# A value projection as seven products and a written order of steps in a two-layer mLSTM and attention trunk

## The chip, the cores and the metric

The kernel runs on one core of a Trainium2 chip. The metric is the device time of one execution in microseconds (us), the median of several runs. TensorE (PE in the profile) multiplies, VectorE (DVE), ScalarE (ACT) and GpSimd (POOL) work on rows of 128 partitions, and SyncE (SP) and GpSimd issue the transfers from HBM.

## The reference, cut to what matters

Two layers, each of three blocks, on 256 tokens of width 1024 in float32; every block ends in a layer norm of the residual sum.

```python
for l in range(2):
    x = layer_norm(ALPHA * x + 0.5 * swiglu(x, ffn_w_in[l, 0], ffn_w_out[l, 0]), ...)   # F = 2816
    y = mlstm_mixer(x, ...) if l == 0 else window_attention(x, ...)
    x = layer_norm(ALPHA * x + y, ...)
    x = layer_norm(ALPHA * x + 0.5 * swiglu(x, ffn_w_in[l, 1], ffn_w_out[l, 1]), ...)

def mlstm_mixer(x, w_in, gate_b, norm_g, w_out):      # 4 heads, q and k 128 wide, v 256 wide
    p = x @ w_in                                      # columns: q 512, k 512, v 1024, o 1024, gates 16
    h = mlstm(q, k, v, gates forward) + mlstm(..., backward)   # decay weights exp(...), read |den| with a floor
    h = normalised per head * norm_g
    return (sigmoid(o) * h) @ w_out
```

The value projection is `x @ w_in[:, 1024:2048]`, the output gate `o` is `x @ w_in[:, 2048:3072]`.

## The kernel before

Every float32 product is made of three float32r matmuls: weights and activations are split in a high part (ScalarE's cast, `w_hi`) and a low part (VectorE's subtraction, `w_lo`), and `mm3` adds hi·hi, hi·lo and lo·hi in one PSUM bank. A word of weights is 128 x 1024; it comes by one transfer of 512 KB and needs one cast on ScalarE and one subtraction on VectorE before TensorE can use it.

The program is written once as a list of steps on tiles without addresses (`Book.note`). `Book.sequence` then plans it: TensorE's steps keep the order in which they were written; the steps of VectorE, ScalarE, GpSimd and of the transfers are picked by due times, with costs from `Book.cost` and a small model of the two transfer rings (`Rings`, `RING`). It also picks the slots of the tiles. `emit` writes the result, one queue in order for each engine; so nearly all rows of the profile have one line, L597, and are told apart by the tiles' names. A step that needs a set of ScalarE's function tables comes behind a `preload` step in the list; after the plan, the lowering puts a table load of its own wherever an activation stands behind a load of another set.

The feed-forward blocks (`ffn`) take most products 512 columns at a time for gate and up part together, as seven products instead of eight (`seven`): words of weights are summed on VectorE or by accumulating transfers from GpSimd's queue (`bring`), sums of the transposed x (`x_one` to `x_four`) are made once, and the seven products `P1`, `P2`, `S1` to `S4`, `A22` share three banks. The strings `FIRST`, `FULL`, `SHUT` and `OPEN` give the order of these steps (`d`, `a` and `b` are products of the down projection and of the rest of 256 columns).

The mLSTM block (`mlstm`) runs in this order: the value projection as 32 groups of three matmuls (`wide_mm`, then `v_evac`), with the transposes of the previous block's second half (`pending`) inside; the gates' projection and their scans; q and k (`narrow`); then for each head `scores`, `mix`, `divide`, `settle`, with the output gate's 32 groups (`gate_units`, counts in `GATE`) between them; `gate_out`, the transposes of the gated h (`to_xT`), and the out projection with the norm (`tail`, `Norm`). ScalarE's tables are loaded in four places there: Exp and Ln ahead of the gates, Sigmoid ahead of the output gate, Silu at the end, and Exp again in the attention block. In this block's names `wt` are the decay weights of a head (six Exp steps of 128 x 128 each), `a` their product with the scores, `den` the denominators, `sg` the sigmoid, `py` and `pw` banks of PSUM.

The attention block (`attn`) follows the string `HEADS`: `P`, `S`, `E`, `N`, `T`, `V` with a pair of heads' number are products, scores, powers, scale, transposes and values, `q*n` and `y0*n`, `y1*n` are n groups of the q projection and of the out projection of each half of the tokens.

Layer norms of the feed-forward blocks other than the last are seeded: ScalarE writes the scaled residual to the bank ahead of the products (`seed`), the products add to it, and ScalarE copies the sum out with a running total (`half`). Mixers and the last block add the residual on VectorE.

Of the kernel before, what the change touches and what calls it, by code (L numbers as in the profile page):

```python
# [27 lines left out]
SUMS = {(2, 0): "23", (5, 0): "23"}  # L28
# [221 lines left out]
class Book:  # L250
# [170 lines left out]
    def sequence(self):  # L421
# [54 lines left out]
        while len(given) < len(steps):  # L476
# [124 lines left out]
def trunk_kernel(ctx: ExitStack, tc: tile.TileContext, x, ffn_w_in, ffn_w_out, ln_g, ln_b, ml_w_in, ml_gate_b,  # L601
# [156 lines left out]
    class Norm:  # L758
        def __init__(self, t, ca, eps, last=False, seeded=False):
            self.t, self.ca, self.eps, self.last, self.seeded = t, ca, eps, last, seeded  # L760
            if last:
# [4 lines left out]
            if not last:
                self.sums = small("sums", [128, 6])
# [58 lines left out]
    def tail(y, h, todo, first, norm, last, turn_at, between=None):  # L826

        def one(t, o, n):
            c, get = todo[t][n]
# [31 lines left out]
        return lambda: emit_x(1, last)  # L861

    def ffn(l, i, n, pending, last):
# [68 lines left out]
        xs, f1 = {}, {}  # L932

        def x_sum(name, a, op, b):
            f = temp(name).rearrange("p (k m) -> p k m", k=4)
            nc.vector.tensor_tensor(f, a, b, op=op)
            v = nc.tile(name, (128, 2, 4, 128), "wide" if name in ("S1", "S2") else "big", FR)
            xs[name] = (v[:, 0], v[:, 1])
            split_evac(xs[name], f)
            return f  # L940

        def x_one():
            f1["x"] = temp("x10").rearrange("p (k m) -> p k m", k=4)
            nc.scalar.copy(f1["x"], turned[1, 0])
            f1["S1"] = x_sum("S1", f1["x"], OP.subtract, turned[1, 1])

        def x_two():
            f1["S2"] = x_sum("S2", f1["S1"], OP.subtract, turned[0, 0])

        def x_three():  # L950
            x_sum("S3", turned[0, 0], OP.subtract, f1["x"])

        def x_four():
            x_sum("S4", turned[0, 1], OP.add, f1["S2"])

# [659 lines left out]
```

## Time and profile before

| what | value |
|---|---|
| time, median of 3 runs | 906.04 us (904.73 to 907.65) |
| profiled execution: time, span | 904.83 us, 903.1 us |
| PE busy | 892.5 us, 99% |
| DVE, ACT, POOL busy | 815.9 us (90%), 635.1 us (70%), 157.8 us (17%) |
| transferred | 216.92 MB, mean 240 GB/s |
| granted TensorE clock | 0.999 |
| ScalarE table loads | 6, 1283 ns each |

The span runs from the first to the last instruction. Matmuls are pipelined and their ends are modelled, so a PE that reads as busy can still have stood for up to a few tenths of a us: such stops show in the starts of the rows, since a 128 x 512 matmul follows the one before by 0.227 us. By the starts, the blocks begin at about 0, 173, 299, 453, 637 and 722 us, and the last matmul starts at 895.4 us.

### The profile page before, as it was taken

The page shows a single profiled execution, that of the slowest core. Times are in us where ns is not written, and L with a number is a line of the kernel's source. Part 1 is how long each engine was busy: PE and PEld are TensorE (multiplying, and loading weights), DVE is VectorE, ACT ScalarE, POOL GpSimd, SP SyncE. Part 2 cuts the span into 40 slices and gives each one's busy share as a digit, 9 for nine tenths or more (in the row PEclk, how much of TensorE's full clock was granted, in tenths as well). Part 3 has the DMA queues.
Part 4 walks back from the last instruction along what each step waited for, and adds up shares of the span by engine and source line. Part 5 has one row for each costly group of instructions (what it writes and reads, how often), then busy time and mean ns, then how long its engine had stood idle before and what let it go on. Part 6 is the DMA issues. An engine that isn't in the chain of part 4 may idle for free.

```text
span 903.1 us, 12618 instructions
## 1 busy us (share of the span) xinstructions
PE 892.5 (99%) x4387; PEld 744.3 (82%) x4387; DVE 815.9 (90%) x1008; ACT 635.1 (70%) x881; POOL 157.8 (17%) x194
## 2 busy tenths in 40 slices
PE   9999999999999999999999999999999999999996
PEld 7888888889988888888888888887898788888885
DVE  7999998678797999999879999996889899999975
ACT  7777677657665886776679776776788777677650
POOL 0121221014012221112011221131033131112100
PEclk9999999999999999999999999999999999999999
DMA  9999998844395989999966999999534588999931
GB/s 317 380 306 273 274 317 243 293 141 141 119 315 149 212 241 316 300 249 278 363 185 177 244 291 322 295 258 347 168 113 113 168 191 230 306 267 263 307 90 46
DMA packets 106111, 216.92 MB, mean 240 GB/s; under 512 B 7192, under 2 KB 23600, under 8 KB 106048
## 3 DMA queue, kind: packets, MB, share of 16 engines
q1 hardware_dynamic: 84000, 174.09, 54.6%
q0 software_dynamic: 22048, 42.04, 27.1%
q8 instruction: 34, 0.56, 0.2%
q14 instruction: 29, 0.24, 0.1%
HBM read 215.04 MB, written 1.05 MB: 239 GB/s over the span
## 4 chain that ended last, share of the span: by engine, by line
PE 73%; DVE 11%; issue 9%; DMA 5%; ACT 1%; POOL 1%; DVEq 0%; POOLq 0%; ACTq 0%
PE pw L597 45%; PE py L597 28%; DVE w_lo L597 5%; DMA b<-in_ffn_w_in_dram 5%; DVE b L597 2%; DVE x L597 1%; DVE e L597 1%; ACT w_hi L597 1%; POOL b L597 1%; POOL rs L597 1%; DVE S L597 0%; DVE xT_lo L597 0%; DVE pv L597 0%; DVE sc L597 0%; DVE h_lo L597 0%
## 5 line engine op out<-in xcount | busy, mean ns | idle before, releaser
L597 ACT CAST w_hi<-b 128x1024 fp32r<-128x1024 f32 x266 | 277.6, 1053 | 98.6 <-PE py L597 45.4
L597 DVE TENSOR_TENSOR w_lo<-b,w_hi 128x1024 fp32r<-128x1024 f32 x266 | 317.5, 1220 | 9.9 <-ACT w_hi L597 9.8
L597 DVE TENSOR_TENSOR w_lo<-raw,w_hi 128x1024 fp32r<-128x1024 f32 (+1 forms) x158 | 187.4, 1208 | 10.5 <-ACT w_hi L597 9.1
L597 PE MATMUL pw<-w_hi,S 128*128 128x512 f32 x608 | 195.3, 391 | 0.2 <-ACT e L597 0.2
L597 ACT CAST w_hi<-raw 128x1024 fp32r<-128x1024 f32 (+1 forms) x158 | 163.2, 1042 | 44.3 <-PE py L597 19.1
L597 POOL DMA_DIRECT2D b<-in_ffn_w_in_dram x80 | 97.0, 1218 | 497.4 <-DVE b L597 173.8
L597 PE MATMUL pw<-w_hi,xT_hi 128*128 128x512 f32 (+1 forms) x420 | 164.9, 394 | 0.4 <-ACT xT_hi L597 0.4
L597 PE MATMUL pw<-w_hi,xT_lo 128*128 128x512 f32 (+1 forms) x420 | 162.4, 388 | 0.0
L597 PE MATMUL pw<-w_lo,xT_hi 128*128 128x512 f32 (+1 forms) x420 | 161.2, 387 | 0.0
L597 PEld LDWEIGHTS pw<-w_hi,S 128*128 128x128 f32 x608 | 114.2, 188 | 25.0 <-ACT e L597 0.7
L597 PE MATMUL py<-w_hi,h_hi 128*128 128x512 f32 x317 | 125.7, 397 | 0.0
L597 PE MATMUL py<-w_hi,h_lo 128*128 128x512 f32 x317 | 124.0, 391 | 0.6 <-DVE h_lo L597 0.6
L597 PE MATMUL py<-w_lo,h_hi 128*128 128x512 f32 x317 | 123.5, 390 | 0.0
L597 PE MATMUL pw<-w_lo,S 128*128 128x512 f32 x304 | 118.4, 390 | 0.0
L597 PEld LDWEIGHTS pw<-w_hi,xT_lo 128*128 128x128 f32 x420 | 78.9, 188 | 18.3 <-DVE xT_lo L597 2.1
L597 PEld LDWEIGHTS pw<-w_hi,xT_hi 128*128 128x128 f32 x420 | 79.0, 188 | 16.2 <-ACT xT_hi L597 1.4
L597 PEld LDWEIGHTS pw<-w_lo,xT_hi 128*128 128x128 f32 x420 | 78.9, 188 | 14.6
L597 DVE TENSOR_TENSOR b<-b,b 128x1024 f32<-128x1024 f32 x72 | 87.7, 1221 | 0.7
L597 PEld LDWEIGHTS py<-w_hi,h_lo 128*128 128x128 f32 x317 | 59.5, 188 | 13.7 <-DVE h_lo L597 1.0
L597 PEld LDWEIGHTS py<-w_lo,h_hi 128*128 128x128 f32 x317 | 59.7, 188 | 11.8
L597 PEld LDWEIGHTS py<-w_hi,h_hi 128*128 128x128 f32 x317 | 59.6, 188 | 11.6
L597 PEld LDWEIGHTS pw<-w_lo,S 128*128 128x128 f32 x304 | 57.1, 188 | 11.6
(205 smaller groups left out, 1102.3 us busy)
## 6 DMA issues: line engine op xcount, KB each, us to landing
b<-in_ffn_w_in_dram SPq DMA_DIRECT2D x152, 512.0 KB, 7.9
raw<-in_ffn_w_out_dram SPq DMA_DIRECT2D x88, 512.0 KB, 8.2
b<-in_ffn_w_in_dram POOLq DMA_DIRECT2D x80, 512.0 KB, 8.8
raw<-in_ml_w_in_dram SPq DMA_DIRECT2D x24, 512.0 KB, 8.0
raw<-in_ffn_w_in_dram SPq DMA_DIRECT2D x36, 256.0 KB, 6.3
raw<-in_at_w_in_dram SPq DMA_DIRECT2D x12, 512.0 KB, 8.6
raw<-in_ml_w_out_dram SPq DMA_DIRECT2D x8, 512.0 KB, 4.5
raw<-in_at_w_out_dram SPq DMA_DIRECT2D x8, 512.0 KB, 8.4
```

Source lines behind the costliest of these rows:

```text
L597: getattr(engines[s.engine], s.name)(*[real(x) for x in s.args], **{k: real(x) for k, x in s.kw.items()})
```

## The change

Five edits:

1. `seven` is cut into a function `strassen` that both `ffn` and `mlstm` use. The value projection becomes one block of seven products over all 1024 columns, with sums of x from `sums_of_x`. Two of the word sums come by accumulating transfers (`SUMS`, entry `(1, 0)`), two on VectorE; four more words are brought by accumulating transfers.
2. The mLSTM's steps follow a string `MIXES`. The output gate's first 16 groups (`u`) move to the front, among the value products; their result is copied out unchanged and passed through Sigmoid later (`sig`). The q and k groups are taken head pair by head pair, and scores and mixes start inside them.
3. `Norm` is seeded in the mixers too (attention: the first half of the tokens) and in the last block for the first half.
4. `HEADS`, `SHUT` and `OPEN` are changed in a few places.
5. Constants of the plan: `RING`, a new `SPARE` added to landing times, `SUMMED`, and costs of some steps.

```diff
-SUMS = {(2, 0): "23", (5, 0): "23"}
+SUMS = {(1, 0): "01", (2, 0): "23", (5, 0): "23"}
-HEADS = ('... E7 y0*2 N7 y0*1 V5 y1*1 '
-         'T60 T61 y0*1 y1*1 V6 y1*1 T70 y1*1 T71 y1*1 V7 y0*1 y1*1 y0*3')
+HEADS = ('... E7 y0*2 '
+         'N7 V5 y1*1 T60 T61 y0*2 y1*1 V6 T70 y1*1 T71 y1*2 V7 y0*1 y1*1 y0*3')
-GATE = [4, 4, 4, 4, 4, 10, 2]
+MIXES = ('P1*2 u*4 P2*2 u*2 p u*2 x1 u*4 x3 g x2 u*4 x4 S1*2 S2*2 S4*2 S3*2 q*7 A22*2 q*1 c q*29 '
+         'sig q*1 H0 q*2 H1 q*8 M0 q*16 u*2 H2 M1 u*1 H3 u*3 M2 u*2 M3 u*8')
-SHUT = "P1*2 d T1 P2*2 S1*2 S2*2 d S3*2 S4*2 d A22*2 T0"
+SHUT = "P1*2 d T1 P2*2 S1*2 S2*2 d*2 S3*2 S4*2 A22*2 T0"
-RING = {"SP": (2000.0, 600.0), "POOL": (2900.0, 1500.0)}
+RING = {"SP": (2000.0, 1250.0), "POOL": (2900.0, 1150.0)}
+SPARE = {"SP": 300.0, "POOL": 1500.0}
-SUMMED = 163.0
+SUMMED = 170.0
...
             if s.name.startswith("preload"):
-                s.takes = 1290.0
+                s.takes = 1450.0
...
-                        steps[n_].lands = t_
+                        steps[n_].lands = t_ + SPARE[steps[n_].engine]
...
     class Norm:
-        def __init__(self, t, ca, eps, last=False, seeded=False):
+        def __init__(self, t, ca, eps, last=False, seeded=True):
+            self.parted = last and t
+            self.seeded = seeded and not self.parted
...
     def mlstm(l, n, pending, last):
...
-        wide_mm(ps[0], 0, wv, 0)
-        v_evac(0, 0, ps[0])
...
+        todo_ = strassen(ml_w_in[0], 1024, 1536, SUMS.get((bound[0], 0), ""), xs, out_(0, 0), out_(0, 1), out_(1, 0), out_(1, 1))
...
+        def gates():
+            nc.scalar.preload_act_table_set("natural_log_exp_and_others")
...
+        def sigm(t, m, ps):
+            if m == 0:
+                nc.scalar.copy(sg[t][:, 0], ps)
+            else:
+                nc.scalar.activation(sg[t][:, 1], ps, AF.Sigmoid)
...
+            if f == 1 and k == 7:
+                hs = slice(2 * g, 2 * g + 2)
+                if m == 0:
+                    split_evac(pair(qT, A, hs), p)
+                else:
+                    split_evac(pair(kT, A, hs), p, 128 ** -0.5)
+                weights(2 * g + m)
...
+        def sigmoids():
+            nc.scalar.preload_act_table(AF.Sigmoid)
+            for t in range(2):
+                nc.scalar.activation(sg[t][:, 0], sg[t][:, 0], AF.Sigmoid)
...
+        run(MIXES, todo_)
         for m in range(2):
             gate_out(0, m)
         to_xT(0, flat[0])
-        gate_units(GATE[6])
+        gate_units(len(units))
...
-        norm = [Norm(t, ALPHA, LN_EPS, last) for t in range(2)]
+        norm = [Norm(t, ALPHA, LN_EPS) for t in range(2)]
+        for t in range(2):
+            for o in range(2):
+                norm[t].seed(o, y[t][o])
...
     def attn(l, n, pending, last):
+        norm = [Norm(t, ALPHA, LN_EPS, seeded=not t) for t in range(2)]
```

In `MIXES`, `weights(2)` and `weights(3)` belong to the q groups 48 and 64, and `sig` stands behind group 37.

The first place is ScalarE's queue around the four heads of the mLSTM. Before, from the last decay weights to the first head's `a_hi`:

```order
L597 ACTIVATE k_hi<-pw 128x512
L597 ACTIVATE wt<-wt,ucol 128x128 x6
L597 ACT_TABLE_LOAD
L597 ACTIVATE w_hi<-raw,few 128x1024 x2
L597 ACTIVATE k_hi<-pw 128x512
L597 ACTIVATE w_hi<-raw,few 128x1024
L597 CAST a_hi<-wt 128x768
```

All decay weights stood ahead of one load of Sigmoid's table there. Now, from the first head's `a_hi` on:

```order
L597 CAST a_hi<-wt 128x768
L597 ACT_TABLE_LOAD x2
L597 ACTIVATE wt<-wt,ucol 128x128 x6
L597 CAST q_hi<-pw 128x512
L597 ACTIVATE den<-py 128x1 x2
L597 ACT_TABLE_LOAD
L597 ACTIVATE sg<-sg 128x512
```

The weights of the third head moved behind the load of Sigmoid's table. The same queue goes on to the second `k_hi`, which the third head's scores read:

```order
L597 ACTIVATE den<-py 128x1
L597 ACTIVATE w_hi<-raw,few 128x1024
L597 CAST a_hi<-wt 128x768
L597 ACTIVATE den<-py 128x1
L597 ACTIVATE w_hi<-raw,few 128x1024
L597 ACTIVATE sg<-sg 128x512
L597 ACT_TABLE_LOAD
L597 ACTIVATE wt<-wt,ucol 128x128 x3
L597 ACTIVATE h_2419<-py,den 128x256
L597 ACTIVATE h_2425<-py,den 128x256
L597 ACTIVATE wt<-wt,ucol 128x128 x3
L597 ACTIVATE k_hi<-pw 128x512
```

From `a_hi` to this `k_hi` there are four table loads now, and a fifth stands behind, ahead of the second half's sigmoid; in the whole program there are ten where there were six.

The second place is TensorE at the end of the mLSTM, where the first half of h is transposed (`py<-ident,h`) and the out projection (`py<-w_hi,xT_hi`) begins. Before:

```order
L597 MATMUL py<-ident,h_2375 128x128 x8
L597 MATMUL pw<-w_hi,xT_hi 128x512
L597 MATMUL pw<-w_lo,xT_hi 128x512
L597 MATMUL pw<-w_hi,xT_lo 128x512
L597 MATMUL pw<-w_hi,xT_hi 128x512
L597 MATMUL pw<-w_lo,xT_hi 128x512
L597 MATMUL pw<-w_hi,xT_lo 128x512
L597 MATMUL py<-w_hi,xT_hi 128x512
L597 MATMUL py<-w_lo,xT_hi 128x512
L597 MATMUL py<-w_hi,xT_lo 128x512
```

And now:

```order
L597 MATMUL pw<-w_hi,xT_hi 128x512
L597 MATMUL pw<-w_lo,xT_hi 128x512
L597 MATMUL pw<-w_hi,xT_lo 128x512
L597 MATMUL py<-ident,h_2419 128x128 x8
L597 MATMUL py<-w_hi,xT_hi 128x512
L597 MATMUL py<-w_lo,xT_hi 128x512
L597 MATMUL py<-w_hi,xT_lo 128x512
```

The last two groups of the output gate (`pw`, six matmuls) moved from behind the transposes to ahead of them.

The third place is TensorE at the last pair of heads of the attention, between its last transposes (`pw<-ident,sc`) and its values (`pw<-pr,v`). Before:

```order
L597 MATMUL pw<-ident,sc 128x128 x4
L597 MATMUL py<-w_hi,q_hi 128x512
L597 MATMUL py<-w_lo,q_hi 128x512
L597 MATMUL py<-w_hi,q_lo 128x512
L597 MATMUL pw<-pr_6932,v_6068 128x512 x2
L597 MATMUL pw<-pr_6952,v_6165 128x512 x2
```

And now:

```order
L597 MATMUL pw<-ident,sc 128x128 x4
L597 MATMUL py<-w_hi,q_hi 128x512
L597 MATMUL py<-w_lo,q_hi 128x512
L597 MATMUL py<-w_hi,q_lo 128x512
L597 MATMUL py<-w_hi,q_hi 128x512
L597 MATMUL py<-w_lo,q_hi 128x512
L597 MATMUL py<-w_hi,q_lo 128x512
L597 MATMUL pw<-pr_6986,v_6122 128x512 x2
L597 MATMUL pw<-pr_6998,v_6220 128x512 x2
```

One more group of the out projection moved in between.

More of the change, by code (lines that the diff above doesn't have):

```diff
@@ L824, in emit_x, with tail @@
             to_xT(t, xt[t])
-    def tail(y, h, todo, first, norm, last, turn_at, between=None):
+    def tail(y, h, todo, norm, last, turn_at, between=None):
         def one(t, o, n):
@@ L830, in one @@
             end = n == len(todo[t]) - 1 or last and t == o == 1 and n == len(todo[t]) // 2 - 1
-            mm3(y[t][o], h(c, t), pair(get(), A, 0, slice(o * 512, o * 512 + 512)), first and n == 0, end, norm[t].seeded)
+            mm3(y[t][o], h(c, t), pair(get(), A, 0, slice(o * 512, o * 512 + 512)), False, end, norm[t].seeded)
         for o in range(2):
@@ new lines, in run, with product, step @@
+    def run(order, todo_):
+        for one in order.split():
+            name, _, n_ = one.partition("*")
+            for _ in range(int(n_ or 1)):
+                todo_[name].pop(0)()
+    def product(b, x_of, parts, first, done):
+        def step(j):
+            w = parts[j]()
+            for k in range(2):
+                mm3(b, x_of(2 * j + k), pair(w, A, k), first and j == k == 0, j == k == 1, not first)
+            if j:
+                done()
+        return [lambda: step(0), lambda: step(1)]
@@ L930, in b_mul @@
             return hh
[L932 to L954, printed above, removed]
+        xs, (x_one, x_two, x_three, x_four) = sums_of_x()
         sevens = SEVENS[bound[0]]
@@ L993, in ffn @@
                 hs[t] = b_mul(sg, ps[1])
-        norm = [Norm(t, 2 * ALPHA, 4 * LN_EPS, last, not last) for t in range(2)]
+        norm = [Norm(t, 2 * ALPHA, 4 * LN_EPS, last) for t in range(2)]
         def down(n_):
@@ L999, in down @@
                 y.extend([bank(name="py") for _ in range(2)] for _ in range(2))
-                if not last:
-                    for t in range(2):
+                for t in range(2):
+                    if norm[t].seeded:
                         for o in range(2):
@@ L1008, in down @@
                     for o in range(2):
-                        mm3(y[t][o], pair(hT[c], A, tok(t)), pair(w, A, 0, slice(o * 512, o * 512 + 512)), last and c == 0, False, not last)
+                        mm3(y[t][o], pair(hT[c], A, tok(t)), pair(w, A, 0, slice(o * 512, o * 512 + 512)), not norm[t].seeded and c == 0, False, norm[t].seeded)
                 done_[0] += 1
         done_ = [0]
-        def product(b, x_of, parts, first, done):
-            def step(j):
-                w = parts[j]()
-                for k in range(2):
-                    mm3(b, x_of(2 * j + k), pair(w, A, k), first and j == k == 0, j == k == 1, not first)
-                if j:
-                    done()
-            return [lambda: step(0), lambda: step(1)]
@@ L1113, in seven @@
-            return todo_, lambda: tr(hB, 1, e["e5"])
-        def run(order, todo_):
-            for one in order.split():
-                name, _, n_ = one.partition("*")
-                for _ in range(int(n_ or 1)):
-                    todo_[name].pop(0)()
+            todo_ = strassen(wi, c0, F + c0, SUMS.get((bound[0], g), ""), xs, silu("e1"), c12, silu("g1"), c22)
+            todo_.update(T0=[turn0], d=[lambda: down(1)] * 4)
+            return todo_, lambda: tr(hB, 1, e["e5"])
         ps = [bank(), bank()]
@@ L1290, in mlstm @@
                     split_evac(pair(kT, A, hs), p, 128 ** -0.5)
-                weights(2 * m + g)
+                weights(2 * g + m)
+        todo_.update(q=[lambda i=(g, m, f, k): qk(*i) for g in range(2) for m in range(2) for f in range(2) for k in range(8)],
+                     u=[lambda: gate_units(1)] * 32, p=[pending], g=[gates], c=[columns], sig=[lambda: sigmoids()],
+                     x1=[sums[0]], x2=[sums[1]], x3=[sums[2]], x4=[sums[3]])
         am = {}
```

336 lines of the change are left out of this document (167 added, 169 removed), and 4 rows, old and new, of the table HEADS.

## The prediction

> **What bounds the kernel now.** I read the page's busy shares first, then the chain that ended last, then a table by stage.
>
> ```profile
> span 903.1 us, 12618 instructions
> PE 892.5 (99%) x4387; PEld 744.3 (82%) x4387; DVE 815.9 (90%) x1008; ACT 635.1 (70%) x881; POOL 157.8 (17%) x194
> PE 73%; DVE 11%; issue 9%; DMA 5%; ACT 1%; POOL 1%; DVEq 0%; POOLq 0%; ACTq 0%
> ```
>
> TensorE is busy for 99% of the span, and the chain is TensorE for 73%. VectorE at 90% is the second bound. By stage (length, then busy time of PE, PEld, DVE, ACT and POOL, the clock, the DMA share): the mLSTM, the feed-forward block behind it, and what follows the last matmul.
>
> ```profile
> 172.80:298.90 126.10, 126.10 (x726) 110.49 (x725) 101.35 (x164) 80.54 (x138) 27.50 (x35) 1.00 0.56 171
> 298.90:452.70 153.80, 153.80 (x702) 127.37 (x701) 149.06 (x150) 113.67 (x136) 24.14 (x20) 1.00 0.99 285
> 895.60:903.10 7.50, 0.08 (x1) 0.00 (x0) 4.00 (x9) 0.00 (x0) 0.99 (x1) 0.85 0.19 70
> ```
>
> TensorE fills its stages at full clock. So a matmul removed is worth its cadence, and a stop of TensorE is lost time; all else lies beside it. The cadence comes from the chain (twelve 128x512 matmuls in 2.72 us) and from the timeline (24 matmuls of 256 or 258 columns start from 249.49 until the next kind starts at 252.36):
>
> ```profile
> 50.16 2.72 PE py L597 x12
> 249.49 0.28 PE L597 MATMUL pw<-q_hi,k_hi 128*128 128x256 f32 x1
> ...
> 252.36 0.40 PE L597 MATMUL pw<-w_hi,xT_hi 128*128 128x512 f32 x1
> ```
>
> That is 0.227 us and 0.120 us. The profiled execution took 904.83 us (span 903.1 and 1.7 around it); the median is 1.2 above it, which I add at the end.
>
> **1. Fewer products.** The value projection goes from 32 groups of three (96 matmuls) to seven products of twelve (84). 12 x 0.227 = 2.7 us less, certain in size: **-2.7**.
>
> **2. Table loads among the heads.** The rows are ScalarE's from the last decay weights on, and TensorE's first score.
>
> ```profile
> 227.77 1.86 ACT L597 ACTIVATE wt<-wt,ucol 128x128 f32<-128x128 f32 x6
> 229.64 1.28 ACT L597 ACT_TABLE_LOAD   x1
> 230.94 2.30 ACT L597 ACTIVATE w_hi<-raw,few 128x1024 fp32r<-128x1024 f32 x2
> 233.15 0.58 ACT L597 ACTIVATE k_hi<-pw 128x512 fp32r<-128x512 f32 x1
> ...
> 236.85 0.84 ACT L597 CAST a_hi<-wt 128x768 fp32r<-128x768 f32 x1 [0.74 <-DVE wt L597]
> ...
> 240.31 0.84 ACT L597 CAST a_hi<-wt 128x768 fp32r<-128x768 f32 x1
> 241.05 0.43 ACT L597 ACTIVATE den<-py 128x1 f32<-128x1 f32 x2
> ...
> 248.13 0.84 ACT L597 ACTIVATE h<-py,den 128x256 f32<-128x256 f32 x2 [1.03 <-DVE den L597]
> ...
> 249.69 0.60 ACT L597 ACTIVATE sg<-pw 128x512 f32<-128x512 f32 x1 [0.23 <-PE pw L597]
> ```
>
> ```profile
> 234.76 0.28 PE L597 MATMUL pw<-q_hi,k_hi 128*128 128x256 f32 x1
> ```
>
> The first a_hi starts 2.1 us after the first head's first score (236.85 against 234.76). From it to the second `k_hi`, ScalarE's new queue holds, by these rows and less 0.1 where the next row starts inside: two a_hi at 0.74 (1.5), four table loads at 1.30 (5.2; from 229.64 to the next start at 230.94), twelve decay weights at 0.31 (3.7), a q_hi (0.5), four den at 0.2 (0.8), two sigmoids at 0.5 (1.0), two w_hi at 1.1 (2.2) and two h (0.7): 15.6 us. With 2.1 ahead and k_hi's 0.58 behind, the third head can begin 18.3 us after the first. Until there TensorE now has 108 matmuls of 256 or 258 columns and six of 512: 108 x 0.120 + 6 x 0.227 = 14.3 us. So it stands for up to 4.0 us. Three of the four loads are new; with one load alone the run would end 3.9 earlier and TensorE would not stand. Bounds: 4.0 with nothing overlapped, 2.3 if one load (1.3) falls into idle time or goes faster behind another. I take 3.6, nearer the upper end, since nothing in the queue waits on TensorE for long: **+3.6**. Behind k_hi wait two w_hi and the third a_hi; they are late by the same, and so is TensorE, so nothing more is lost.
>
> One page speaks against this edit as a whole. The Trainium skill, "ScalarE: Activation LUTs", section "What ACT_TABLE_LOAD costs", gives 1283 ns for a load and 1380 ns of drain, 2.66 us for each switch. By that the four loads would hold ScalarE 10.6 us, not 5.2, and the sum would be 5.4 higher. The trace agrees with the 1283 and not with the drain here: the decay weights ended at 229.63, the load began at 229.64 and the next cast at 230.94.
>
> **3. The turn at the end of the mLSTM.** TensorE's last mix and its transposes, then VectorE, then ScalarE:
>
> ```profile
> 257.16 0.29 PE L597 MATMUL py<-v_hi,a_lo 128*128 128x258 f32 x1
> ...
> 264.11 1.04 PE L597 MATMUL py<-ident,h 128*128 128x128 f32 x8
> ```
>
> ```profile
> 262.55 0.69 DVE L597 TENSOR_TENSOR h<-h,sg 128x512 f32<-128x512 f32 x1
> ...
> 265.88 1.29 DVE L597 TENSOR_TENSOR xT_lo<-py,xT_hi 128x512 fp32r<-128x512 f32 x2 [0.25 <-ACT xT_hi L597]
> ```
>
> ```profile
> 265.26 1.07 ACT L597 CAST xT_hi<-py 128x512 fp32r<-128x512 f32 x2
> ```
>
> From the last mix to the gated h are 6.1 us (257.16 to 263.24). Before, ten gate groups were left for it; now eight are, 24 x 0.227 = 5.4 us: 0.6 short. Behind the transposes six gate matmuls (1.4 us) covered the casts; now none do. The first xT_lo ended at about 266.5, 2.4 after the first transpose, and the out projection's third matmul wants it 8 x 0.109 + 2 x 0.227 = 1.3 after (0.109 by the transposes' starts): 1.1 short. Together 1.7. Below, one cast of 1.0 may no longer stand ahead of xT_hi: 0.8. Above, the sigmoid's load (1.28) delays a den in this chain in part: 2.5. I take **+1.6**.
>
> **4. VectorE in the value projection.**
>
> ```profile
> L597 DVE TENSOR_TENSOR w_lo<-raw,w_hi 128x1024 fp32r<-128x1024 f32 x24 | 28.4, 1218 | 4.1 <-ACT w_hi L597 4.1
> L597 DVE SCALAR_TENSOR_TENSOR w_lo<-raw,few,w_hi 128x1024 fp32r<-128x1024 f32 x8 | 10.1, 1279 | 2.9 <-ACT w_hi L597 2.9
> L597 DVE TENSOR_TENSOR xT_lo<-py,xT_hi 128x512 fp32r<-128x512 f32 x10 | 6.4, 687 | 5.3 <-ACT xT_hi L597 5.3
> L597 DVE SCALAR_TENSOR_TENSOR x<-x,py 128x512 f32<-128x512 f32 x4 | 2.7, 685 | 1.3 <-PE py L597 1.3
> L597 DVE TENSOR_TENSOR b<-b,b 128x1024 f32<-128x1024 f32 x2 | 2.4, 1222 | 0.0
> L597 POOL DMA_DIRECT2D b<-in_ffn_w_in_dram x80 | 97.0, 1218 | 497.4 <-DVE b L597 173.8
> ```
>
> New are six w_lo (7.3), two word sums (2.4), four sums of x and four of their low parts (8 x 0.69 = 5.5) and two subtractions at the products' end (1.4): 16.6. The four residual sums (2.7 and their totals) go: 13.6 net. 101.35 becomes 115 in a stage that keeps 126.1 - 2.7 = 123.4 us: 93%. The nearest row is the next block, where VectorE is at 149.06 of 153.80, 97%, and TensorE does not stop. Ends: 0 by that row, 3.8 by rival B; I take **+0.5**, near the block that runs the same steps. ScalarE's six casts, four sums' casts and copies (some 13 us on 80.5) leave it at 76%, the next block's 74%. The six new accumulating transfers cost GpSimd 6 x 1.22 = 7.3 us of issue on 27.5, and the rings stand at 56% against 99% in a block without stops: 0, up to one issue (1.2) if a sum lands late.
>
> **5. Attention's stops.** In TensorE's starts between 620 and 722 some twelve gaps exceed the cadence, 4.3 us together. The first, the largest and the last:
>
> ```profile
> 620.15 0.39 PE L597 MATMUL py<-w_lo,h_hi 128*128 128x512 f32 x1
> 621.14 0.50 PE L597 MATMUL py<-w_hi,h_lo 128*128 128x512 f32 x1 [0.60 <-DVE h_lo L597]
> ...
> 706.67 1.25 PE L597 MATMUL pw<-pr,v 128*128 128x512 f32 x3
> 708.15 0.50 PE L597 MATMUL pw<-pr,v 128*128 128x512 f32 x1 [0.23 <-DVE pr L597]
> ...
> 721.33 0.40 PE L597 MATMUL py<-w_hi,q_lo 128*128 128x512 f32 x1
> 721.89 0.50 PE L597 MATMUL pw<-w_hi,xT_hi 128*128 128x512 f32 x1 [0.16 <-ACT xT_hi L597]
> ```
>
> At 708.15 TensorE is 0.80 late (706.67 + 3 x 0.227 = 707.35): the last head's values wait for `pr`. One more group (0.68) now stands ahead, which closes most of it. The stops at 621 and 721 (0.76 and 0.33) hang on the plan's order of casts, which the new constants shift. Ends 0 and -4.3; about half: **-2.0**.
>
> **6. Seeds and the strings.** The mixers' residual goes from VectorE (0.685) to a seed on ScalarE, and the sum is copied out there:
>
> ```profile
> L597 ACT ACTIVATE x<-py 128x512 f32<-128x512 f32 x12 | 7.2, 602 | 9.7 <-PE py L597 9.7
> L597 ACT ACTIVATE py<-x 128x512 f32<-128x512 f32 x12 | 6.6, 598 | 0.0
> ```
>
> The copy takes 0.60 where the sum took 0.69, and a total's read on either side; the seed runs ahead, when ScalarE (70%) has room. The last half of the last block keeps its old norm, so the 7.5 us behind the last matmul stay. **0**, within 0.4 for four halves (4 x 0.09). The feed-forward strings keep their matmuls: 0, under VectorE's 97% without a stop.
>
> **Sum.** -2.7 + 3.6 + 1.6 + 0.5 - 2.0 = +1.0: 905.8 for the profiled execution, **907.0 us** as the median. This kernel's measurement tells 0.3% (2.7 us) from no change: 903.3 to 908.8 counts as the same.
>
> **Rivals.** A (faster): the third head does not wait. For it: ScalarE's idle time before is large (70% busy), and the first a_hi may start earlier; against it: the run of 15.6 us is back to back by count. 907.0 - 3.6 = 903.4.
> B (slower): VectorE becomes the bound. Before it idled 4.1 + 2.9 + 5.3 = 12.3 us in this stage behind ScalarE's casts; now only 123.4 - 115.0 = 8.4 are left for that. If those waits all stay, the stage is 3.9 too short: 907.0 - 0.5 + 3.9 = 910.4. It decides once VectorE's waits exceed 8.4. Against it: the next block idles only 4.7.
> C (slower): each of the four loads holds ScalarE twice its 1.28: 907.0 + 4 x 1.28 = 912.1. The 0.01 us ahead of the load and the 0.02 behind it (229.64 + 1.28 = 230.92) speak against it. This is near what the Trainium skill's section above would make of the loads.
> D: the plan's constants do nothing and attention's stops stay: 907.0 + 2.0 = 909.0. For it: a stop at 621 hangs on a split of VectorE, which nothing relieves.
>
> **Chances.** The forecast 53% (904 to 909.5 by its terms' ends: faster 6, same 34, slower 13), A 22% (faster 13, same 9), B 14%, C 3% (both slower), D 8% (same 4, slower 4): faster 19, same 47, slower 34. The range 901.0 to 912.0 reaches to A with attention's stops gone in full (903.4 - 2.3 = 901.1) and to B with the turn at its upper end; about 12% lies outside.
>
> **What would show it.** Ten table loads; a gap of about 3.6 us ahead of the third head's first score, with k_hi as what ended it; a gap of 0.6 and one of 1.1 around the transposes at the end of the mLSTM; 84 value products; VectorE near 93% there; a smaller gap ahead of the last `pw<-pr,v`. No gap at the third head makes step 2 wrong and the time 3.6 less; a row of gaps of VectorE's w_lo among the value products makes step 4 wrong.

## The result: 916.4 us, slower by 1.1%, and the profile after

The changed kernel takes 916.44 us (median of 4 runs, 913.84 to 917.04) against 906.1: a ratio of 1.0112 (95% interval 1.0088 to 1.0136). The forecast was 907.0, in a range of 901.0 to 912.0. One run of e9 below was taken at a granted clock of 0.655 (1273.6 us) and is left out of its median. These lines of the page after answer to those shown of before:

```profile
span 914.4 us, 12652 instructions
PE 893.3 (98%) x4375; PEld 744.0 (81%) x4375; DVE 825.4 (90%) x1011; ACT 659.7 (72%) x927; POOL 163.6 (18%) x200
PE 71%; DVE 14%; issue 7%; ACT 4%; DMA 3%; POOL 1%; DVEq 0%; POOLq 0%; ACTq 0%
```

The span grew by 11.3 us and TensorE's busy time only by 0.8: TensorE stands. The mLSTM by stretches (columns as in the prediction): to the gates' product, to the first head's scores, to the first transposes of h, to the end:

```profile
172.80:203.00 30.20, 29.99 (x149) 24.71 (x148) 25.37 (x33) 23.21 (x36) 6.17 (x9) 1.00 0.52 119
203.00:231.80 28.80, 28.80 (x184) 26.05 (x182) 27.19 (x37) 18.08 (x26) 5.69 (x6) 1.00 0.74 214
231.80:275.60 43.80, 34.97 (x225) 31.61 (x224) 32.49 (x69) 34.33 (x73) 10.37 (x18) 0.96 0.52 174
275.60:310.00 34.40, 32.85 (x156) 27.02 (x155) 27.89 (x37) 23.20 (x36) 7.62 (x6) 1.00 0.73 205
```

The third stretch is where TensorE is idle, 34.97 busy of 43.80, and its clock fell to 0.96. In the second, VectorE is at 27.19 of 28.80.

To count stops I add, over all of TensorE's rows, the gap from one start to the next less the cadence of the first (0.227, 0.120 and 0.109 us as in the prediction; 0.064 for the hundred on 64 rows, of which most start in pairs). In these sums the matmuls fell from 880.0 to 877.3 us; the excess over the cadence rose from 0.9 to 15.2 us in 175 to 300, fell from 6.9 to 4.9 in 600 to 725 (attention and the end of the block ahead of it), and rose by 1.8 elsewhere. -2.7 + 14.3 - 2.0 + 1.8 = 11.4, the growth of the span but for rounding. The 14.3 lie at five places:

| place | excess, us |
|---|---|
| ahead of the first head's scores, and the slow matmuls behind | 6.0 |
| ahead of the third head's scores | 3.0 |
| in the mixes of the third and fourth head | 2.8 |
| the turn at the end of the mLSTM | 2.0 |
| a value product at 196, behind the copy of the transposed x | 0.5 |

TensorE at the first head; the gap is 235.79 - 231.76 less 0.12, 3.9 us:

```profile
231.76 0.28 PE L597 MATMUL pw<-xT_hi,w_lo 128*128 128x256 f32 x1
235.79 0.38 PE L597 MATMUL pw<-q_hi,k_hi 128*128 128x256 f32 x1 [3.75 <-ACT k_hi L597]
...
236.90 0.41 PE L597 MATMUL pw<-q_hi,k_hi 128*128 128x256 f32 x1
237.11 0.41 PE L597 MATMUL pw<-q_lo,k_hi 128*128 128x256 f32 x1
```

It waits for k_hi. Behind the stop the starts are 0.213 apart instead of 0.120, up to 239.67: half speed for some 3 us, 1.4 us lost. Why k_hi is late stands in ScalarE's rows:

```profile
224.16 0.59 ACT L597 CAST q_hi<-pw 128x512 fp32r<-128x512 f32 x1 [0.51 <-PE pw L597]
231.06 2.74 ACT L597 ACTIVATE wt<-wt,ucol 128x128 f32<-128x128 f32 x9 [6.31 <-POOL wt L597]
233.70 0.60 ACT L597 CAST v_hi<-e 128x512 fp32r<-128x512 f32 x1
234.21 1.04 ACT L597 CAST w_hi<-raw 128x1024 fp32r<-128x1024 f32 x1
235.16 0.58 ACT L597 ACTIVATE k_hi<-pw 128x512 fp32r<-128x512 f32 x1
```

ScalarE stood 6.31 us for GpSimd's broadcast of the decay weights, with k_hi behind nine of them in its queue. GpSimd in turn:

```profile
220.10 1.18 POOL L597 DMA_DIRECT2D most<-scan  x2 [16.57 <-ACT w_hi L597]
227.82 4.04 POOL L597 PARTITION_BROADCAST wt<-most  x3 [6.54 <-issue]
```

It got the scan's result at 220, while before the same transfer was issued at 206 and the first head began at 234.76, not 231.8. The scan itself is VectorE's; its first and last row before, and after:

```profile
198.06 0.47 DVE L597 SCALAR_TENSOR_TENSOR scan<-pw,few,gl 32x256 f32<-32x256 f32 x1 [1.01 <-ACT gl L597]
...
206.47 0.42 DVE L597 SCALAR_TENSOR_TENSOR scan<-scan 64x256 f32<-64x256 f32 x1
```

```profile
203.04 0.47 DVE L597 SCALAR_TENSOR_TENSOR scan<-pw,few,gl 32x256 f32<-32x256 f32 x1
...
220.25 0.42 DVE L597 SCALAR_TENSOR_TENSOR scan<-scan 64x256 f32<-64x256 f32 x1
```

The chain of the scan, fifteen steps of VectorE, took 8.4 us before and 17.2 now, because other steps stand between its own: eight low parts of words (six of the value projection's), one of a sum of x and one subtraction, where one low part stood before. These 8.8 us are not all: the scan ends 13.8 us later. Another 3.8 come from the gates' product, which the scan reads and which stands later in TensorE's order (before, and after), and 1.2 from the steps ahead of the scan on VectorE:

```profile
195.54 0.28 PE L597 MATMUL pw<-xT_hi,gw 128*128 128x256 f32 x1
```

```profile
199.32 0.28 PE L597 MATMUL pw<-xT_hi,gw 128*128 128x256 f32 x1
```

No run moved the gates' product alone, so the share of each is read from the rows and not shown by an experiment. The other three places, in TensorE's rows:

```profile
254.60 0.39 PE L597 MATMUL pw<-q_hi,k_hi 128*128 128x256 f32 x1 [2.26 <-ACT k_hi L597]
...
264.24 0.36 PE L597 MATMUL py<-v_hi,a_hi 128*128 128x258 f32 x1 [0.75 <-DVE wt L597]
...
268.92 0.39 PE L597 MATMUL py<-v_hi,a_hi 128*128 128x258 f32 x1 [1.62 <-ACT h L597]
...
277.12 0.63 PE L597 MATMUL py<-ident,h 128*128 128x128 f32 x4 [0.92 <-DVE h L597]
...
278.83 0.50 PE L597 MATMUL py<-w_hi,xT_lo 128*128 128x512 f32 x1 [0.62 <-DVE xT_lo L597]
```

### The profile page after: what moved, and what is told of

Its sections match the earlier page's. It is cut to its first block, busy times and chain, and to the rows that moved or that the text cites. A ratio compares the mean times of both kernels' runs of the same rounds, so it can differ in the third digit from the quotient of the medians.

```text
span 914.4 us, 12652 instructions
## 1 busy us (share of the span) xinstructions
PE 893.3 (98%) x4375; PEld 744.0 (81%) x4375; DVE 825.4 (90%) x1011; ACT 659.7 (72%) x927; POOL 163.6 (18%) x200
## 4 chain that ended last, share of the span: by engine, by line
PE 71%; DVE 14%; issue 7%; ACT 4%; DMA 3%; POOL 1%; DVEq 0%; POOLq 0%; ACTq 0%
PE pw L597 44%; PE py L597 26%; DVE w_lo L597 7%; DMA b<-in_ffn_w_in_dram 2%; DVE b L597 1%; DMA raw<-in_ffn_w_out_dram 1%; ACT sc L597 1%; DVE e L597 1%; ACT L597 1%; ACT wt L597 1%; ACT w_hi L597 1%; DVE x L597 1%; DVE pr L597 0%; DVE h L597 0%; DVE pv L597 0%
## 5 line engine op out<-in xcount | busy, mean ns | idle before, releaser
L597 ACT CAST w_hi<-b 128x1024 fp32r<-128x1024 f32 x280 | 291.8, 1053 | 104.4 <-PE py L597 48.3
L597 DVE TENSOR_TENSOR w_lo<-b,w_hi 128x1024 fp32r<-128x1024 f32 x280 | 334.4, 1219 | 10.5 <-ACT w_hi L597 10.0
L597 PE MATMUL pw<-w_hi,S 128*128 128x512 f32 x640 | 205.8, 391 | 0.2 <-DVE h_lo L597 0.2
L597 DVE TENSOR_TENSOR w_lo<-raw,w_hi 128x1024 fp32r<-128x1024 f32 (+1 forms) x150 | 178.8, 1208 | 10.9 <-ACT w_hi L597 9.9
L597 ACT CAST w_hi<-raw 128x1024 fp32r<-128x1024 f32 (+1 forms) x150 | 155.1, 1041 | 36.0 <-PE pw L597 15.6
L597 PE MATMUL pw<-w_hi,xT_hi 128*128 128x512 f32 (+1 forms) x400 | 157.2, 395 | 1.4 <-DVE h_lo L597 1.0
L597 PE MATMUL pw<-w_hi,xT_lo 128*128 128x512 f32 (+1 forms) x400 | 154.8, 389 | 0.0
L597 PE MATMUL pw<-w_lo,xT_hi 128*128 128x512 f32 (+1 forms) x400 | 153.4, 386 | 0.0
L597 PEld LDWEIGHTS pw<-w_hi,S 128*128 128x128 f32 x640 | 120.1, 188 | 26.6 <-DVE h_lo L597 1.6
L597 PE MATMUL pw<-w_lo,S 128*128 128x512 f32 x320 | 124.5, 389 | 0.0
L597 PEld LDWEIGHTS pw<-w_hi,xT_hi 128*128 128x128 f32 x400 | 75.3, 189 | 17.2 <-DVE h_lo L597 1.8
L597 PEld LDWEIGHTS py<-w_lo,h_hi 128*128 128x128 f32 x317 | 59.6, 188 | 11.8
```

What stands on the lines that cost most here:

```text
L597: getattr(engines[s.engine], s.name)(*[real(x) for x in s.args], **{k: real(x) for k, x in s.kw.items()})
```

## The experiments

The table gives each run's median, its ratio to the kernel before in the same comparison, and, from its one profiled execution, the span and the excess of TensorE's starts in the mLSTM, in attention and elsewhere. The matmuls' own sum is 880.0 us in the kernel before, e4 and e5, and 877.3 in the others. A profiled execution can lie some us off the median (e8), so places are read from the excess and verdicts from the ratio.

| run | time, us | ratio (95%) | span | mLSTM | attention | elsewhere |
|---|---|---|---|---|---|---|
| before | 906.1 | 1 | 903.1 | 0.9 | 6.9 | 6.4 |
| the change | 916.4 | 1.0112 (1.0088 to 1.0136) | 914.4 | 15.2 | 4.9 | 8.2 |
| e1_sig_late | 916.3 | 1.0127 (1.0104 to 1.0149) | 913.8 | 12.6 | 6.4 | 8.6 |
| e2_lib | 923.0 | 1.0195 (1.0175 to 1.0216) | 920.0 | 21.9 | 3.8 | 8.1 |
| e3_lib_sig | 919.8 | 1.0161 (1.0144 to 1.0178) | 917.9 | 20.4 | 4.6 | 6.8 |
| e4_eight | 918.7 | 1.0147 (1.0130 to 1.0164) | 916.8 | 8.0 | 3.9 | 16.0 |
| e5_plan | 911.8 | 1.0070 (1.0046 to 1.0094) | 908.7 | 1.1 | 5.1 | 13.6 |
| e6_late_sig | 908.1 | 1.0026 (1.0013 to 1.0039) | 909.3 | 7.3 | 4.6 | 11.2 |
| e7_v3 | 915.4 | 1.0110 (1.0080 to 1.0139) | 916.8 | 13.0 | 8.1 | 9.6 |
| e8_v4 | 909.3 | 1.0036 (1.0018 to 1.0053) | 905.1 | 5.2 | 7.1 | 6.7 |
| e9_late | 910.2 | 1.0064 (1.0048 to 1.0080) | 910.1 | 9.8 | 5.8 | 8.4 |
| e10_v5 | 910.4 | 1.0055 (1.0041 to 1.0068) | 908.5 | 7.3 | 6.8 | 8.2 |
| e11_v6 | 908.6 | 1.0037 (1.0025 to 1.0050) | 907.2 | 7.4 | 4.7 | 9.1 |
| e12_v7 | 910.5 | 1.0058 (1.0045 to 1.0071) | 910.2 | 8.3 | 7.0 | 8.9 |
| e13_scans | 915.8 | 1.0110 (1.0094 to 1.0126) | 914.2 | 10.3 | 7.9 | 9.9 |
| e14_scans_late | 908.4 | 1.0030 (1.0018 to 1.0041) | 909.3 | 6.5 | 8.7 | 7.9 |
| e15_best1 | 910.4 | 1.0044 (1.0031 to 1.0057) | 910.7 | 5.8 | 8.1 | 10.7 |
| e16_best2 | 912.8 | 1.0073 (1.0057 to 1.0090) | 911.7 | 8.3 | 8.1 | 9.2 |

**Table loads alone: e1_sig_late.**

```diff
-... c q*29 sig q*1 H0 q*2 H1 q*8 M0 q*16 u*2 H2 ...
+... c q*29 q*1 H0 q*2 H1 q*8 M0 q*16 sig u*2 H2 ...
```

> The changed kernel with one word of MIXES moved: sig stands behind the last q group, so all decay weights are ahead of Sigmoid's load. Queue theory (the time is lost in ScalarE's and GpSimd's queues at the heads, not to VectorE's load): six table loads, the stop of 3.0 us ahead of the third head's scores gone, the one of 4.6 us ahead of the first head unchanged within 1 us; time 916.4 - 3.0 = 913.4, between 911.5 and 915. Rival (VectorE's load in the value products makes scans and all that hangs on them late): the third head's stop stays over 2 us and the time is 915 to 917.5.

Six loads, as expected, and the third head's scores wait 0.4 us and not 2.4 (start to start 251.35 to 251.98, less 0.23):

```profile
251.98 0.38 PE L597 MATMUL pw<-q_hi,k_hi 128*128 128x256 f32 x1 [0.24 <-ACT k_hi L597]
```

The mLSTM's excess fell by 2.5, but the time did not fall and missed the forecast (at most 915): a stop of 1.6 us opened at 625, far from the edit, since every edit makes the planner order all queues anew. So the loads' price at this place is shown by the trace; by itself it buys nothing.

**The planner told of GpSimd's long starts: e2_lib, and with the edit above e3_lib_sig.**

```diff
+            if s.name in ("partition_broadcast", "tensor_tensor"):
+                if s.name != getattr(self, "library", "tensor_tensor"):
+                    s.takes += 6500.0
+                self.library = s.name
```

> The changed kernel, with 6.5 us added to the planner's cost of GpSimd's first partition broadcast and of the first power behind the broadcasts (the trace shows about 7 us before each); the program is the same, the queues' order is planned anew: k_hi and its low part stand ahead of the first decay weights on ScalarE. The four table loads among the heads stay. Queue theory: the first head's stop falls from 4.6 us to under 1, but ScalarE's run to the second k_hi keeps its loads, so the third head's stop grows from 3.0 to 4 to 6; the stops at the mixes (2.8 us together) fall as VectorE no longer stands at the head scale; time 911 to 915. Rival (VectorE's load): the scans are not earlier by this, the first head's stop stays over 3 us, time 915 to 917.

> The edits of the two runs before together. Queue theory: stops ahead of the first and the third head under 1 us each, those at the mixes between 0 and 2.8; 916.4 - 4.2 - 2.6 - 1.4 = 908, between 906 and 910. Rival (VectorE's load): 913 to 916.

Both missed. The first head's scores no longer wait (k_hi stands ahead of the weights), but its mix then waits 2.3 us, and the planner, which now took GpSimd's powers for late, put the heads' last scaling behind five other steps on VectorE. In e3 TensorE stood 6.3 and 2.9 us at the turn, and the matmuls behind ran at 0.427 instead of 0.227:

```profile
PE py L601 <- DVE h L601: 8.6, 2, 6.1
PE py L601 <- ACT a_hi L601: 3.3, 2, 2.3
```

**The rival of VectorE's load, first try: e4_eight.** Value groups `v` of three matmuls come in place of the seven products and their sums.

```diff
-MIXES = ('P1*2 u*4 P2*2 u*2 p u*2 x1 u*4 x3 g x2 u*4 x4 S1*2 S2*2 S4*2 S3*2 q*7 A22*2 q*1 c q*29 '
+MIXES = ('v*14 p v*2 g v*16 u*16 q*7 q*1 c q*29 '
```

> The changed kernel with the value projection as 32 groups of three again (96 matmuls, no sums of x on VectorE, no accumulating transfers for it), ahead of the output gate's first 16 groups; all from the first q group on stands as in the change. Queue theory: the heads' stops of 12 us together stay within 3 us, and the twelve matmuls come back: 916.4 + 2.7 = 919, between 916 and 921. Rival (VectorE's load): the heads' stops fall under 5 us in all, 916.4 - 8 + 2.7 = 911, between 908 and 913.

The time agrees with the first theory; the trace is nearer the rival. The mLSTM's excess is 8.0, not 15.2, the heads' stops 5.7 us and not 11.8 (the rival asked for under 5), and 6.5 us of the time are a new stop at 138, in the feed-forward block ahead. The scan's chain took 11.5 us (205.13 to 216.65) instead of 17.2, and the first head waited 1.1. So the chain on VectorE does belong to the cause; the total alone would have misled. But the edit also moves the gates' product 3.2 us forward in the block and the first head 2.2 us back, so it does not price VectorE's load alone.

**The constants and `HEADS` on the kernel before: e5_plan.**

```diff
-RING = {"SP": (2000.0, 600.0), "POOL": (2900.0, 1500.0)}
+RING = {"SP": (2000.0, 1250.0), "POOL": (2900.0, 1150.0)}
+SPARE = {"SP": 300.0, "POOL": 1500.0}
... (HEADS, SUMMED and the costs of steps as in the change)
```

> The kernel before with the new HEADS and all new constants of the plan (RING, SPARE, SUMMED, the costs of steps), nothing else. Theory: attention's stops shrink by 2.0 us as in the changed kernel and nothing else moves: 906.0 - 2.0 = 904.0, between 902.5 and 905. Rival (the constants shift the order elsewhere and open stops in feed-forward blocks): attention falls by 2 in the trace, but a stop over 1 us opens elsewhere and the time is 905.5 or more.

The rival held. Attention's excess fell from 6.9 to 5.1, and at 138 a product waited for a low part on VectorE:

```profile
137.63 0.39 PE L596 MATMUL py<-w_hi,h_lo 128*128 128x512 f32 x1
141.99 0.80 PE L596 MATMUL pw<-w_hi,xT_hi 128*128 128x512 f32 x1 [3.96 <-DVE h_lo L596]
```

The stop and the half-speed matmuls behind it cost 6.8 us. It is not in the changed kernel; the constants belong to one program's plan.

**The first head later: e6_late_sig, and without moving sig e9_late.**

```diff
-... c q*29 sig q*1 H0 q*2 H1 q*8 M0 q*16 u*2 H2 ...
+... c q*41 q*1 H0 q*2 H1 q*8 M0 q*4 sig u*2 H2 ...
```

> The changed kernel with two moves in MIXES: twelve more q groups (4.3 us) ahead of the first head, and sig behind the last q group. Theory (decay weights come late behind VectorE's scans and GpSimd's broadcasts, so the first head stands too early): the first head's stop falls from 3.9 us to under 1 and the half-speed matmuls behind it vanish, the third head's stays under 1, the mixes and the turn keep their 4.8: 916.4 - 4.2 - 2.4 = 910, between 908 and 912.5. Rival (ScalarE's run through the heads is the bound, wherever TensorE stands): the stops move to the third head and the mixes, the sum of stops between the first head and the transposes stays over 9 us, time 914 or more.

> The changed kernel with the twelve q groups ahead of the first head alone; sig stays ahead of the first head, so table loads stay among the heads (nine in all, three of them added where a load of another set stood ahead). Beside the run that had both moves (908.1) this prices the loads where the first head no longer waits. Theory: the loads hold the second k_hi and the head's casts: 908.1 + 2 to 4 = 911, between 909.5 and 913, with a stop of over 1.5 us ahead of the third head or its mix. Rival (with the first head late, the loads lie beside other work): 907 to 909.

Both as expected. With twelve q groups more ahead, no stop stands ahead of the first head, and of the 10.3 us that the change lost, 8 are back. The largest stops left in the mLSTM are at the first mix, 1.8 and 0.8 us with 1.6 lost in half-speed matmuls behind, and the turn's 1.3. At the first mix it is VectorE that comes late to the product of decay weights and scores: it stands behind low parts, with no idle time before it.

```profile
243.83 0.36 PE L596 MATMUL py<-v_hi,a_hi 128*128 128x258 f32 x1 [1.60 <-issue]
244.99 0.40 PE L596 MATMUL py<-v_hi,a_lo 128*128 128x258 f32 x1 [0.68 <-DVE a_lo L596]
```

```profile
240.52 1.42 DVE L596 SCALAR_TENSOR_TENSOR w_lo<-raw,few,w_hi 128x1024 fp32r<-128x1024 f32 x1
241.86 1.01 DVE L596 TENSOR_TENSOR wt<-pw,wt 128x512 f32<-128x512 f32 x2
```

In e9 sig stays ahead and there are eight loads (nine were expected); TensorE stands 1.9 us ahead of the third head again, and the ratio is 1.0064 against 1.0026.

```profile
250.35 0.39 PE L597 MATMUL pw<-q_hi,k_hi 128*128 128x256 f32 x1 [1.79 <-ACT h L597]
```

That stop is not the loads' price, though. e11 below has e6's `MIXES`, six loads and ScalarE's rows at the heads in e6's order, and waits 1.5 us there too:

```profile
250.41 0.39 PE L596 MATMUL pw<-q_hi,k_hi 128*128 128x256 f32 x1 [1.35 <-ACT h L596]
```

From the first head's first score to this head's `k_hi` it is 13.3 us in e6 and in e11 and 13.7 in e9. So the loads hold `k_hi` by 0.4 us; e6 did not wait because its half-speed matmuls had already held TensorE for as long. The kernel as a whole is 2 to 3 us slower in e9, and what of that the loads cost is not shown. Where the first head is not moved, e1 does show a price: the third head begins 16.7 us after the first there, and 18.8 in the change.

**More q ahead, other covers: e7_v3, e8_v4, e10_v5, e12_v7.** The edits are strings behind `c`; e7 and e8 also have all four word sums by transfers and the old feed-forward strings.

```diff
+e7:  q*45 q*1 H0 q*4 H1 q*6 M0 sig u*3 H2 M1 u*2 H3 u*3 M2 u*2 M3 u*6
+e8, e12:  q*55 q*1 sig H0 u*2 H1 u*2 M0 u*2 H2 M1 u*2 H3 M2 M3 u*8
+e10: q*45 q*1 H0 q*2 H1 q*8 M0 sig u*2 H2 M1 u*2 H3 u*2 M2 u*2 M3 u*6
```

> The run before with four more q groups ahead of the first head, six between the second and the first mix, three gate groups ahead of the third head, two gate groups left behind the transposes, all four word sums of the value products by accumulating transfers (2.4 us less of VectorE) and the feed-forward strings of before. Theory: stops at the heads under 3 us in all, the turn under 1, no stop of 1.1 us at 860: 916.4 - 12 + 3 - 1 - 1.2 = 905, between 903 and 908. Rival (ScalarE's run is the bound): 910 or more.

> The changed kernel with all q groups ahead of the first head and sig ahead of it, the eight gate groups between the heads two by two, the word sums by transfers and the feed-forward strings of before. Theory: no stop ahead of the first head, but only 8 x 0.68 = 5.4 us cover the four heads (13.6 before), each with about 4 us from scores to mix: stops of 3 to 7 us at mixes: 909, between 906 and 912. Rival (VectorE's load in the value products holds everything behind it): a stop ahead of the first head's mix of over 3 us remains.

> All moves of q in one: sixteen more q groups ahead of the first head (5.8 us), none between the first mix and the third head, sig behind the last q group, gate groups two by two, two left behind the transposes at the turn. Theory: the 2.6 us that the first mix still waited in the run with twelve fall by 1.4 (four groups of 0.36), the turn's 1.3 fall under 0.7, the later mixes lose cover of 1.4: about 907, between 905 and 909.5. Rival (ScalarE's run is the bound): the stops move to the third head's mix, 910 or more.

> The changed kernel with MIXES alone replaced: all q groups ahead of the first head, sig behind them, eight gate groups two by two between the heads, eight behind the last mix. Word sums and feed-forward strings as in the change. Theory: the heads' stage loses 3 to 5 us in stops where the change lost 14; attention keeps its 2 us and the products their 2.7: 916.4 - 10 = 906.5, between 904.5 and 909. Rival (VectorE's load in the value products holds what is behind): 911 or more.

e8 came out as expected; e7, e10 and e12 missed by 10, 3 and 4 us. By their times e7 and e10 are where the rival (ScalarE's run as the bound) had them, at 910 or more, but their largest stops are at other places. In e10 the first head and its mix are clear (0.4), but the turn waits 2.6 us for h: two gate groups taken from ahead of the transposes are missed there. In e7 the second head's scores wait 3.8 us for a q_lo that the new plan put late on VectorE, and 2.6 us went at 617. In e12 the first mix waits 2.7 us, and in e10 and e12 stops of 1.9 opened at 620.

**The feed-forward strings: e11_v6** is e6 with `SHUT` and `OPEN` of the kernel before (the diff shows the first).

```diff
-SHUT = "P1*2 d T1 P2*2 S1*2 S2*2 d*2 S3*2 S4*2 A22*2 T0"
+SHUT = "P1*2 d T1 P2*2 S1*2 S2*2 d S3*2 S4*2 d A22*2 T0"
```

> The run with both moves (908.1) with SHUT and OPEN as before. Theory: the stop of 1.3 us at about 855 (a down product's low part late behind VectorE's sums) belongs to the new SHUT and goes: 908.1 - 1.4 = 906.7, between 905 and 908. Rival: the stop is the plan's, not the string's, and stays or comes back at another place: 908 or more.

The stop of 1.3 at 855 went and one of 1.5 at 821 came: the rival held.

**Order or load: e13_scans; with e6's string e14_scans_late.** The scan's transfer is due 20 us earlier, so VectorE runs fourteen of the scan's fifteen steps in a row (202.11 to 209.47), all that the transfer and the decay weights need.

```diff
+            if s.name == "dma_start" and s.outs and s.outs[0].room.name == "most":
+                s.due -= 20000.0
```

> The changed kernel with one thing added to the plan: the transfer of the running maxima to GpSimd's side is due 20 us earlier, so VectorE does the whole scan as soon as the gates' product is there and the sums and low parts of value words wait. MIXES as in the change; two of the table loads fall away with the new order (eight, two of them back to back). Order theory: decay weights come some 10 us earlier, the first head's stop of 4.6 falls under 1, the third head's under 1.5, and the value products, late by less than their slack, open less than 1.5 us of stops: 916.4 - 6 = 910, between 907.5 and 912. Load theory (VectorE at 90% has no room): stops of 4 us or more open among the value products between 203 and 232, time 914 or more.

> The run with the first head twelve q groups later and sig behind q (908.1), with the scans first as well. Order theory: the 2.6 us that its first mix still waited for decay weights go, the turn's 1.3 and the small stops stay: 905.5, between 904 and 907. Load theory: stops in the value products take their place, 908 or more.

The stops and the time came out as the load theory had them. In e13 the transfer went out at 209 instead of 220. But the sums of x are late by what the scan took:

```profile
209.47 0.39 PE L599 MATMUL pw<-w_hi,S 128*128 128x512 f32 x1
212.63 0.50 PE L599 MATMUL pw<-w_hi,S 128*128 128x512 f32 x1 [2.78 <-ACT S L599]
...
213.72 1.22 PE L599 MATMUL pw<-w_hi,S 128*128 128x512 f32 x2 [0.35 <-DVE S L599]
```

With the half-speed matmuls behind, that is 5.2 us in place of 6.0, and the stretch from 203 to 232 reads so:

```profile
203.00:232.00 29.00, 25.87 (x141) 21.93 (x140) 27.19 (x36) 20.24 (x32) 13.71 (x13) 0.94 0.70 196
```

VectorE is at 27.19 of 29.00 here too. So here the scan does not go first without holding the products. What an early transfer would have gained, e13 does not show: the first head waits only 0.6 us, but not because its weights are early. They also read `ucol`, which TensorE transposes behind the value products, and TensorE came there 5.5 us later; so the weights began 2.1 us and not 11 us earlier, and with two table loads behind them `k_hi` came 1.4 us later than in the change (235.16).

```profile
227.52 0.29 DVE L599 COPY ucol<-pw 128x128 f32<-128x128 f32 x1
228.98 0.98 ACT L599 ACTIVATE wt<-wt,ucol 128x128 f32<-128x128 f32 x3
236.58 0.57 ACT L599 ACTIVATE k_hi<-pw 128x512 fp32r<-128x512 f32 x1
```

That VectorE's work is what leaves no room is borne out by e16 below, where the planner takes the scan early too and all four word sums come by transfers, 2.4 us less for VectorE: the transfer goes out at 210 and the value products lose 0.1 us. The planner's order differs there as well, so the two are not parted in full. e14 moves the wait from the first mix to the value products (0.7 and 1.3 us, and half-speed matmuls) and ends where e6 did.

**Both with the rest: e15_best1** (e14's string with `M3 u*6` and the old feed-forward strings) **and e16_best2** (e8 with the scans first).

> The run before with two gate groups left behind the transposes at the turn and the feed-forward strings of the kernel before. Order theory: the turn's 1.3 us fall under 0.6 or turn into a longer wait for h by as much (two groups less ahead), the stop at 855 goes: 904.5, between 903 and 907. Load theory: 908 or more.

> All q groups ahead of the first head (909.3 before), with the scans first. Order theory: with decay weights early, the stops at the first mix go (1.0 of them), those of the later mixes stay (2.5): 907, between 905 and 909.

Both missed, e15 where the load theory had it (908 or more): the turn waits 1.9 us in e15, the first mix 2.5 in e16 (VectorE comes to its product at 244.76, behind four low parts, though all weights are done by 236.5), and stops of 0.8 to 2.6 us stand between 610 and 630 in both. No version here beats the kernel before; e6 comes nearest, 0.26% above it (0.13 to 0.39).

## Why the prediction was wrong, step by step

- **Step 1** (-2.7, fewer products): -2.7.
- **Step 2** (+3.6, the third head): 3.0, with k_hi as what ended it and ten loads; the third head begins 18.8 us after the first, 18.3 were added up. But the step took the first head's start as given and counted ScalarE's run from there. That is the omission: the first head now stands 26 q groups earlier in TensorE's order, and the step did not ask whether its decay weights come as early. They cost 6.0 us and were not in the sum.
- **Step 3** (+1.6, the turn): 2.0, as a stop of 1.1 for h (0.6 forecast) and one of 0.9 for xT_lo (1.1 forecast), the two that were named.
- **Step 4** (+0.5, VectorE at 93% in the value projection) is the step that failed. It had VectorE's work about right (112.9 us measured, 115 added up). But the nearest row, a block at 97% without stops, was read as proof that 93% is free, and a stop was looked for only among the products. That block has no scan; here the fifteen small steps of the scan have to end in the same stretch, which took them 17.2 us in place of 8.4, and they start a chain over a transfer, GpSimd and ScalarE that made the first head's weights and k_hi late. The products themselves lost 0.5 us, as forecast; the chain behind the scan paid. Rival B had the mechanism (VectorE has more to do than the stage leaves room for) with 14%, and looked for it among the value products. That the first head stands too early for its inputs is shown by e6 and e9, where it stands twelve groups later and the stop ahead of its scores is gone; that VectorE has no room for the scan beside the products, by e13 with its stops and e16 without them. How much of the lost time is VectorE's load and how much the later gates' product stays open.
- **Not in any step**: 2.8 us in the third and fourth head's mixes. GpSimd's power for the head norm came 7.1 us after its last select, and VectorE stood 2.88 us at the scaling behind it, with the fourth head's products and the reads that free the mixes' banks behind it in its queue. Before, GpSimd idled 16.17 us at this place, and the lateness was hidden.

```profile
261.66 0.73 POOL L597 TENSOR_TENSOR hrs<-hrs,few 128x2 f32<-128x2 f32 x1 [7.12 <-issue]
262.43 0.74 DVE L597 TENSOR_SCALAR h<-h,hmv,hrs 128x256 f32<-128x256 f32 x2 [2.88 <-POOL hrs L597]
```

  That the lateness reaches TensorE by this way is read from the waits; no run took GpSimd's long start away, so it is not shown by an experiment.
- **Step 5** (-2.0, attention): -2.0 in the changed kernel. Ahead of the last values the stop of 0.80 is gone: 705.61 follows 705.38 by 0.23, and the four run without a wait, as in every run with the new `HEADS`. The other 1.2 us are luck: in those runs the stage's excess lies anywhere between 3.8 and 8.7, above the 6.9 of before in seven of seventeen, so "about half" was a guess that the plan happened to meet.

```profile
705.38 0.39 PE L597 MATMUL py<-w_hi,q_lo 128*128 128x512 f32 x1
705.61 1.23 PE L597 MATMUL pw<-pr,v 128*128 128x512 f32 x4
```

- **Step 6** (0): +1.8 outside the two stages, 1.25 of it one stop at 860 that e11 could move but not remove.

So steps 1 and 3 held, step 2 to within its bounds and step 5 in its number. The span grew by 11.3 us where 1.0 was forecast; of the 10.3 between them, 6.0 and 2.8 are the two that were in no sum and 1.8 is step 6.

## What to carry to other kernels

When steps of the engine that bounds are moved ahead, follow each of their inputs back to its source and date it anew; a wait that was hidden by what stood between is the first thing the move uncovers. A busy share over a stage says nothing of a chain with a date inside it: list what the full engine must finish by when. And where a planner orders everything anew after each edit, judge an edit by its own place in the trace and by the total, since stops of 1 to 7 us open elsewhere by chance of the plan.

## What was unexpected of the hardware

TensorE's clock can fall after a stop (the third stretch above has a granted clock of 0.96). After the 3.9 us at the first head some fourteen matmuls started 0.213 apart (0.120 before), and after the 4.1 us in e5 twelve started 0.427 apart (0.227), 1.4 and 2.6 us on top of the stops; after the 2.4 us at the third head none did. The Trainium skill, "TensorE: Matmul & The Clock Gate", Part 1, puts the clock at half after an idle window of about 3.4 us and back after about as much work; the runs agree on some 3 to 5 us of slow starts, 1.8 to 1.9 times as far apart. They do not bear out 3.4 us as the least stop: in e6 and in e11 the first mix stood 1.8 and 0.8 us, by the same order of matmuls, and behind it seventeen ran slow in e6 (first) and none in e11 (second).

```profile
245.40 0.42 PE L596 MATMUL py<-v_lo,a_hi 128*128 128x258 f32 x1
245.61 0.42 PE L596 MATMUL py<-v_hi,a_lo 128*128 128x258 f32 x1
```

```profile
244.39 0.28 PE L596 MATMUL py<-v_lo,a_hi 128*128 128x258 f32 x1
244.51 0.28 PE L596 MATMUL py<-v_hi,a_lo 128*128 128x258 f32 x1
```

So one and the same stop can cost 1 to 2 us more in one execution than in another.

GpSimd needs a long start ahead of its first broadcast and again ahead of the first power after the broadcasts: 6.5 and 7.1 us here, between 5.5 and 8.6 in the other runs where the profile names no other wait. The first is 6.0 us from the landing of the transfer that it reads (221.80). The views show no instruction in it; the trace has two short MODIFY_POOL_CONFIG at its head (at 221.30 and 254.57). The Trainium skill, "GPSIMD Engine Reference", section 2.1, states about 6 us of code loading for the first call to a freshly loaded kernel, without a visible instruction; the trace agrees with the size, and shows that going back costs as much.
